# RMS normalization on one core: squares of nine rows at the end of the third slot, gamma in five pieces, and the last tile stored in halves

## Chip, core and metric

The kernel runs on one core of a Trainium2 chip. The metric is the device time of one execution in microseconds (us), the median of several runs. Tile numbers in the code count from 0; and groups are named by the code's pair (tile, first row).

## What is computed

Each row of 512 float32 numbers is divided by the root of its mean square plus 1e-5, and multiplied by gamma.

```python
batch, seq, dim = 16, 1024, 512
x     : float32 [16, 1024, 512]      # 33.55 MB
gamma : float32 [512]

rms = np.sqrt(np.mean(x ** 2, axis=-1, keepdims=True) + 1e-5)
return x / rms * gamma               # 33.55 MB again
```

The 16384 rows are four tiles of 128 partitions x 32 rows x 512 elements, 8.39 MB each. One row on all 128 partitions is 262 KB.

## The kernel before

Three slots of SBUF hold a tile each; the fourth tile goes into the first slot again once the first tile has been stored from there. All transfers are issued by SyncE, in the order in which the code has them.

```python
slots = [const.tile([P, R, D], fp32, name=f"slot{i}") for i in range(3)]
...
pieces = (0, 128, 192, 256, 320, 384, 448, D)

load(0, 0, 0, 8)                       # tile 0, slot 0, rows 0 to 7
for c0, c1 in zip(pieces, pieces[1:]): # seven transfers of gamma
    nc.sync.dma_start(out=gamma_row[:, c0:c1], in_=gamma.unsqueeze(0)[:, c0:c1])
load(0, 0, 8, 16)
load(0, 0, 16, 32)
load(1, 1, 0, 16)
load(1, 1, 16, 32)
```

The work is cut into nine groups: tile, first row, rows, the pieces in which the sums of squares are formed, and the number of rows at the group's end that GpSimd scales.

```python
groups = [
    (0, 0, 7, (7,), 3),
    (0, 7, 9, (4, 5), 5),
    (0, 16, 16, (7, 5, 4), 7),
    (1, 0, 16, (7, 5, 4), 7),
    ...
    (3, 16, 16, (7, 5, 4), 5),
]

def square_sums(ss, t, g, r, m, k):
    # the pieces take turns between a buffer in PSUM (7 rows) and one in SBUF (5 rows)
    home, name, most = ((psum, "sq_psum", 7), (const, "sq_sbuf", 5))[k % 2]
    sq = home.tile([P, most, D], fp32, name=name)
    rows = slots[slot_of[t]][:, g + r : g + r + m, :]
    nc.scalar.activation(out=sq[:, :m], in_=rows, func=AF.Square)
    nc.vector.tensor_reduce(out=ss[:, r : r + m, 0], in_=sq[:, :m], axis=..., op=OP.add)

def inverse_rms(ss, n):                # ScalarE: square root; VectorE: reciprocal
    ...
def scale_by_pool(rstd, t, g, n, share):
    # GpSimd multiplies the group's last rows by 1/rms, then by gamma_b
    ...
def scale(rstd, t, g, r0, r1):         # ScalarE, one row an instruction
    ...
def times_gamma(t, g, r0, r1):         # VectorE multiplies those rows by gamma_psum
    ...
def transfers(t, g):                   # issued when group (t, g) has been recorded
    if (t, g) == (0, 0):
        store(0, 0, 0, 1)
        load(2, 2, 0, 16)
        store(0, 0, 1, 2)
        load(2, 2, 16, 32)
    elif (t, g) == (0, 16):
        store(0, 0, 2, 16)
        store(0, 0, 16, 32)
        load(3, 0, 0, 16)
        load(3, 0, 16, 32)
    elif (t, g) == (1, 16):
        store(1, 1, 0, 32)
    elif (t, g) == (2, 16):
        store(2, 2, 0, 32)
    elif (t, g) == (3, 16):
        store(3, 0, 0, 32)
```

In the loop, the squares of the next group are formed beside the scaling of this one:

```python
for k, group in enumerate(groups):
    ...
    scale_by_pool(rstd, t, g, n, share)
    for piece in todo[:2]:             # of the next group
        square_sums(*piece)
    scale(rstd, t, g, 0, half)
    if not ahead:                      # the last group
        times_gamma(t, g, 0, half)
    for piece in todo[2:]:
        square_sums(*piece)
    scale(rstd, t, g, half, mine)
    times_gamma(t, g, 0 if ahead else half, mine)
    transfers(t, g)
    for nxt in ahead:
        rstd = inverse_rms(ss, nxt[2])
```

In the compiled program each transfer signals one of eight semaphores, which are taken in turn. A transfer's instruction on SyncE waits until the transfer eight places earlier, which has the same semaphore, has landed. SyncE works through its list strictly in order. This is the beginning of the list:

```
load  tile 0 rows 0-7
load  gamma, seven pieces
load  tile 0 rows 8-15      [waits for semaphore 0]
load  tile 0 rows 16-31     [waits for semaphore 1]
load  tile 1 rows 0-15      [waits for semaphore 2]
load  tile 1 rows 16-31     [waits for semaphore 3]
store tile 0 row 0          [waits for semaphore 4, VectorE]
```

Of the kernel before, what the change touches and what calls it, by code (L numbers as in the profile page):

```python
# [9 lines left out]
def kernel(  # L10
# [7 lines left out]
    P = nc.NUM_PARTITIONS  # L18
    eps = 1e-5
    fp32 = mybir.dt.float32  # L20
# [5 lines left out]
    N, D = xf.shape  # L26
# [9 lines left out]
    const = ctx.enter_context(tc.tile_pool(name="const", bufs=1))  # L36
    stats = ctx.enter_context(tc.tile_pool(name="stats", bufs=9))
    psum = ctx.enter_context(tc.tile_pool(name="psum", bufs=1, space=bass.MemoryType.PSUM))

    slots = [const.tile([P, R, D], fp32, name=f"slot{i}") for i in range(3)]  # L40
# [3 lines left out]
    def load(t, slot, r0, r1):  # L44
        dma = nc.sync.dma_start(out=slots[slot][:, r0:r1], in_=xv[t][:, r0:r1])  # L45
        before_scale.append((slot, r0, r1, dma))

    def store(t, slot, r0, r1):
        dma = nc.sync.dma_start(out=ov[t][:, r0:r1], in_=slots[slot][:, r0:r1])  # L49
        before_scale.append((slot, r0, r1, dma))  # L50

    gamma_row = const.tile([1, D], fp32)
    pieces = (0, 128, 192, 256, 320, 384, 448, D)

    load(0, 0, 0, 8)
    for c0, c1 in zip(pieces, pieces[1:]):
# [15 lines left out]
    nc.scalar.activation(out=table, in_=eps_t, func=AF.Sqrt)  # L72


    groups = [
        (0, 0, 7, (7,), 3),
        (0, 7, 9, (4, 5), 5),
        (0, 16, 16, (7, 5, 4), 7),
        (1, 0, 16, (7, 5, 4), 7),
        (1, 16, 16, (7, 5, 4), 7),  # L80
        (2, 0, 16, (7, 5, 4), 7),
        (2, 16, 16, (7, 5, 4), 7),
        (3, 0, 16, (7, 5, 4), 7),
        (3, 16, 16, (7, 5, 4), 5),
    ]
    slot_of = [0, 1, 2, 0]

    def square_sums(ss, t, g, r, m, k):
        home, name, most = ((psum, "sq_psum", 7), (const, "sq_sbuf", 5))[k % 2]
        sq = home.tile([P, most, D], fp32, name=name)  # L90
        rows = slots[slot_of[t]][:, g + r : g + r + m, :]
        nc.scalar.activation(out=sq[:, :m], in_=rows, func=AF.Square)  # L92
        nc.vector.tensor_reduce(  # L93
            out=ss[:, r : r + m, 0], in_=sq[:, :m], axis=mybir.AxisListType.X, op=OP.add
        )

    def inverse_rms(ss, n):
        nc.scalar.activation(out=ss[:, :n, 0], in_=ss[:, :n, 0], func=AF.Sqrt, bias=eps_t, scale=1.0 / D)  # L98
        nc.vector.reciprocal(out=ss[:, :n, 0], in_=ss[:, :n, 0])  # L99
        return ss  # L100

    def scale_by_pool(rstd, t, g, n, share):
        part = slots[slot_of[t]][:, g + n - share : g + n, :]
        by_row = rstd[:, n - share : n].to_broadcast([P, share, D])
        nc.gpsimd.tensor_tensor(out=part, in0=part, in1=by_row, op=OP.mult)  # L105
        last = nc.gpsimd.tensor_tensor(  # L106
            out=part, in0=part, in1=gamma_b.to_broadcast([P, share, D]), op=OP.mult
        )
        before_scale.append((slot_of[t], g + n - share, g + n, last))

    def scale(rstd, t, g, r0, r1):
        x = slots[slot_of[t]]
        for r in range(r0, r1):
            nc.scalar.activation(out=x[:, g + r, :], in_=x[:, g + r, :], func=AF.Copy, scale=rstd[:, r])  # L114

    def times_gamma(t, g, r0, r1):
        part = slots[slot_of[t]][:, g + r0 : g + r1, :]
        scaled = nc.vector.tensor_tensor(  # L118
            out=part, in0=part, in1=gamma_psum.to_broadcast([P, r1 - r0, D]), op=OP.mult
        )  # L120
        for slot, b0, b1, earlier in before_scale:
            if slot == slot_of[t] and b0 < g + r1 and g + r0 < b1:
                tc.declare_no_dep(scaled.ins, earlier.ins, reason="ScalarE waited for it before it scaled these rows")

    def transfers(t, g):
        if (t, g) == (0, 0):
            store(0, 0, 0, 1)
            load(2, 2, 0, 16)
            store(0, 0, 1, 2)
            load(2, 2, 16, 32)  # L130
        elif (t, g) == (0, 16):
            store(0, 0, 2, 16)
            store(0, 0, 16, 32)
            load(3, 0, 0, 16)
            load(3, 0, 16, 32)
        elif (t, g) == (1, 16):
            store(1, 1, 0, 32)
        elif (t, g) == (2, 16):
            store(2, 2, 0, 32)
        elif (t, g) == (3, 16):  # L140
            store(3, 0, 0, 32)

    def pieces_of(group):
        t, g, n, pieces, share = group
        ss = stats.tile([P, 16, 1], fp32, name="ss")
        r = 0
        todo = []
        for k, m in enumerate(pieces):
            todo.append((ss, t, g, r, m, k))
            r += m  # L150
        return ss, todo

    ss, todo = pieces_of(groups[0])
    for piece in todo:
        square_sums(*piece)
    rstd = inverse_rms(ss, groups[0][2])
    nc.scalar.copy(out=gamma_b[:, 0], in_=gamma_psum[:, 0])  # L157
    for k, group in enumerate(groups):
        t, g, n, pieces, share = group
        mine = n - share  # L160
        half = (mine + 1) // 2
        ahead = groups[k + 1 :][:1]
        ss, todo = pieces_of(ahead[0]) if ahead else (None, [])
        scale_by_pool(rstd, t, g, n, share)
        for piece in todo[:2]:
            square_sums(*piece)
        scale(rstd, t, g, 0, half)
        if not ahead:
            times_gamma(t, g, 0, half)
        for piece in todo[2:]:  # L170
            square_sums(*piece)
        scale(rstd, t, g, half, mine)
        times_gamma(t, g, 0 if ahead else half, mine)
        transfers(t, g)
        for nxt in ahead:
            rstd = inverse_rms(ss, nxt[2])
# [30 lines left out]
```

## Time and profile before

| | |
|---|---|
| time, median of 3 runs | 163.77 us (163.73 to 164.01) |
| span of the profiled execution | 162.0 us |
| bytes moved | 67.12 MB, mean 414 GB/s over the span |
| VectorE busy | 111.5 us (69%) |
| ScalarE busy | 107.0 us (66%) |
| GpSimd busy | 110.3 us (68%) |
| TensorE busy | 2.0 us (1%) |

In the profile's lines PE is TensorE, DVE VectorE, ACT ScalarE, POOL GpSimd and SP SyncE; SPq is SyncE's queue of instructions, and L45, L49 and L57 are the lines of the kernel that load, store and fetch gamma. The table of slices cuts the span into 40 equal parts, with the busy share in tenths. In a table of windows, each row is a stretch of time with its length, the busy time of each engine, the granted TensorE clock, the mean busy share of the 16 transfer engines and the GB/s that they moved; a packet is counted where it ends. In a timeline, the first number is the start, the second the time until the last of the merged instructions ended.

### The profile page before, as it was taken

How to read it: one execution, taken by the hardware profiler on the slowest of the kernel's cores; microseconds unless marked ns; L12 is line 12 of the kernel's file. 1: busy time of each engine (PE TensorE's matmuls, PEld its weight loads, DVE VectorE, ACT ScalarE, POOL GpSimd, SP SyncE). 2: the span in 40 equal slices, each digit the busy share in tenths (PEclk: the TensorE clock that was granted, in tenths of full speed). 3: DMA queues.
4: the chain of work that ended last, by engine and by line, in shares of the span. 5: the costliest groups of instructions: out<-in, count | busy, mean ns of one | idle time of the engine just before them, and what ended most of it. 6: DMA issues, size and time to landing. Idle time of an engine off the chain costs nothing.

```text
span 162.0 us, 278 instructions
## 1 busy us (share of the span) xinstructions
PE 2.0 (1%) x2; PEld 0.5 (0%) x2; DVE 111.5 (69%) x43; ACT 107.0 (66%) x109; POOL 110.3 (68%) x24
## 2 busy tenths in 40 slices
PE   0050000000000000000000000000000000000000
PEld 0010000000000000000000000000000000000000
DVE  0027692997989999999999989899998193000000
ACT  3072968878999998999899499999951950000000
POOL 1001947972999599999999999999999994000000
DMA  6789899899899989999999989959959959959974
GB/s 196 324 291 485 388 453 453 388 469 437 316 509 405 453 388 395 446 453 396 510 388 429 477 388 437 599 259 518 518 259 518 518 259 518 518 259 518 518 324 194
DMA packets 2319, 67.12 MB, mean 414 GB/s; under 512 B 269, under 2 KB 270, under 8 KB 526
## 3 DMA queue, kind: packets, MB, share of 16 engines
q1 hardware_dynamic: 2318, 67.11, 97.1%
q14 instruction: 1, 0.01, 0.0%
HBM read 33.56 MB, written 33.55 MB: 414 GB/s over the span
## 4 chain that ended last, share of the span: by engine, by line
DMA 48%; POOL 11%; DVE 10%; ACT 8%; POOLq 4%; issue 2%; SPq 0%; ACTq 0%
DMA slot<-in_x_dram 27%; DMA out_dram<-slot 21%; POOL slot L105 7%; DVE ss L93 5%; POOL slot L106 5%; DVE slot L118 4%; POOLq L202 3%; ACT slot L114 3%; ACT sq_psum L92 3%; ACT sq_sbuf L92 1%; SPq L45 0%; DVE ss L99 0%; SPq L49 0%; POOLq L105 0%; ACTq L92 0%
## 5 line engine op out<-in xcount | busy, mean ns | idle before, releaser
L105 POOL TENSOR_TENSOR slot<-slot,ss 128x3584 f32<-128x3584 f32 (+2 forms) x9 | 48.7, 5407 | 24.0 <-DVE ss L99 24.0
L93 DVE TENSOR_REDUCE ss<-sq_psum 128x7 f32<-128x3584 f32 (+1 forms) x16 | 49.2, 3074 | 18.8 <-ACT sq_psum L92 18.8
L106 POOL TENSOR_TENSOR slot<-slot,gamma_b 128x3584 f32<-128x3584 f32 (+2 forms) x9 | 61.4, 6826 | 0.7
L114 ACT ACTIVATE slot<-slot,ss 128x512 f32<-128x512 f32 x73 | 46.2, 706 | 4.7 <-DVE ss L99 4.7
L92 ACT ACTIVATE sq_psum<-slot 128x3584 f32<-128x3584 f32 (+1 forms) x16 | 40.2, 2512 | 10.6 <-DMA slot<-in_x_dram 9.2
L118 DVE TENSOR_TENSOR slot<-slot,gamma_psum 128x4608 f32<-128x4608 f32 (+3 forms) x10 | 40.3, 4042 | 4.2 <-ACT slot L114 4.2
L93 DVE TENSOR_REDUCE ss<-sq_sbuf 128x5 f32<-128x2560 f32 x8 | 22.5, 2809 | 0.0
L92 ACT ACTIVATE sq_sbuf<-slot 128x2560 f32<-128x2560 f32 x8 | 18.6, 2320 | 0.0
L98 ACT ACTIVATE ss<-ss,eps_t 128x16 f32<-128x16 f32 (+2 forms) x9 | 2.7, 302 | 8.4 <-DVE ss L93 8.4
L99 DVE RECIPROCAL ss<-ss 128x16 f32<-128x16 f32 (+2 forms) x9 | 2.1, 238 | 0.4 <-ACT ss L98 0.4
L66 PE MATMUL gamma_psum<-gamma_row,ones_col 1*128 1x512 f32 x2 | 2.0, 1122 | 9.0 <-DMA gamma_row<-in_gamma_dram 9.0
L72 ACT ACT_TABLE_LOAD x1 | 1.3, 1283 | 1.1 <-PEq L191 1.1
L157 ACT COPY gamma_b<-gamma_psum 128x512 f32<-128x512 f32 x1 | 0.6, 566 | 0.0
L66 PEld LDWEIGHTS gamma_psum<-gamma_row,ones_col 1*128 1x128 f32 x2 | 0.5, 305 | 9.0 <-issue 9.0
L64 POOL MEMSET ones_col<- 1x128 f32 x1 | 0.2, 195 | 0.3 <-POOLq L191 0.3
L191 POOL MEMSET const-float32-0.0<- 128x1 f32 x1 | 0.1, 99 | 0.2 <-issue 0.2
L72 ACT ACTIVATE table<-eps_t 128x1 f32<-128x1 f32 x1 | 0.2, 203 | 0.0
L191 POOL MEMSET const-bfloat16-1.0<- 128x1 bf16 x1 | 0.1, 102 | 0.0
L191 POOL MEMSET const-uint8-127<- 128x1 uint8 x1 | 0.1, 102 | 0.0
L191 POOL MEMSET const-float32-1.0<- 128x1 f32 x1 | 0.1, 99 | 0.0
L70 POOL MEMSET eps_t<- 128x1 f32 x1 | 0.1, 89 | 0.0
## 6 DMA issues: line engine op xcount, KB each, us to landing
slot<-in_x_dram SPq DMA_DIRECT2D x7, 4096.0 KB
slot<-in_x_dram SPq DMA_DIRECT2D x2, 2048.0 KB, 7.3
out_dram<-slot SPq DMA_DIRECT2D x1, 4096.0 KB
out_dram<-slot SPq DMA_DIRECT2D x1, 3584.0 KB, 34.7
out_dram<-slot SPq DMA_DIRECT2D x2, 256.0 KB
gamma_row<-in_gamma_dram SPq DMA_DIRECT2D x6, 0.2 KB
out_dram<-slot SPq DMA_DIRECT2D x3
gamma_row<-in_gamma_dram SPq DMA_DIRECT2D x1, 0.5 KB
```

The lines of the kernel that those rows point to most:

```text
L66: nc.tensor.matmul(gamma_psum[:, 0], ones_col, gamma_row, start=True, stop=True)
L72: nc.scalar.activation(out=table, in_=eps_t, func=AF.Sqrt)
L92: nc.scalar.activation(out=sq[:, :m], in_=rows, func=AF.Square)
L93: nc.vector.tensor_reduce(out=ss[:, r : r + m, 0], in_=sq[:, :m], axis=mybir.AxisListType.X, op=OP.add)
L98: nc.scalar.activation(out=ss[:, :n, 0], in_=ss[:, :n, 0], func=AF.Sqrt, bias=eps_t, scale=1.0 / D)
L99: nc.vector.reciprocal(out=ss[:, :n, 0], in_=ss[:, :n, 0])
L105: nc.gpsimd.tensor_tensor(out=part, in0=part, in1=by_row, op=OP.mult)
L106: last = nc.gpsimd.tensor_tensor(out=part, in0=part, in1=gamma_b.to_broadcast([P, share, D]), op=OP.mult)
L114: nc.scalar.activation(out=x[:, g + r, :], in_=x[:, g + r, :], func=AF.Copy, scale=rstd[:, r])
L118: scaled = nc.vector.tensor_tensor(out=part, in0=part, in1=gamma_psum.to_broadcast([P, r1 - r0, D]), op=OP.mult)
L157: nc.scalar.copy(out=gamma_b[:, 0], in_=gamma_psum[:, 0])
L202: with _tile.TileContext(nc) as tc:
```

## The change

The squares of nine rows at once need 18 KB in each partition, for which there is no buffer. Until the last nine rows of tile 2 are loaded, the end of the third slot is free; the change lets the groups (0,7), (0,16) and (1,0) write squares there, so that each has one piece less, and splits the load of tile 2 so that these rows come after their last use as a buffer. A third row of tile 0 is stored alone ahead of that load. Gamma comes in five pieces. At the end the last tile is stored in two halves, the last group gives GpSimd three rows where it had five, and its multiplication by gamma is one instruction.

```diff
-    pieces = (0, 128, 192, 256, 320, 384, 448, D)
+    pieces = (0, 128, 224, 320, 416, D)
 ...
         (0, 0, 7, (7,), 3),
-        (0, 7, 9, (4, 5), 5),
-        (0, 16, 16, (7, 5, 4), 7),
-        (1, 0, 16, (7, 5, 4), 7),
+        (0, 7, 9, (9,), 5),
+        (0, 16, 16, (7, 9), 7),
+        (1, 0, 16, (7, 9), 7),
 ...
-        (3, 16, 16, (7, 5, 4), 5),
+        (3, 16, 16, (7, 5, 4), 3),
 ...
-        home, name, most = ((psum, "sq_psum", 7), (const, "sq_sbuf", 5))[k % 2]
-        sq = home.tile([P, most, D], fp32, name=name)
+        if m == 9:
+            sq = slots[2][:, 23:32, :]
+        else:
+            home, name, most = ((psum, "sq_psum", 7), (const, "sq_sbuf", 5))[k % 2]
+            sq = home.tile([P, most, D], fp32, name=name)
 ...
             store(0, 0, 0, 1)
             load(2, 2, 0, 16)
             store(0, 0, 1, 2)
-            load(2, 2, 16, 32)
+            load(2, 2, 16, 23)
         elif (t, g) == (0, 16):
-            store(0, 0, 2, 16)
+            store(0, 0, 2, 3)
+            load(2, 2, 23, 32)
+            store(0, 0, 3, 16)
             store(0, 0, 16, 32)
 ...
+        elif (t, g) == (3, 0):
+            store(3, 0, 0, 16)
         elif (t, g) == (3, 16):
-            store(3, 0, 0, 32)
+            store(3, 0, 16, 32)
 ...
         scale(rstd, t, g, 0, half)
-        if not ahead:
-            times_gamma(t, g, 0, half)
         for piece in todo[2:]:
             square_sums(*piece)
         scale(rstd, t, g, half, mine)
-        times_gamma(t, g, 0 if ahead else half, mine)
+        times_gamma(t, g, 0, mine)
```

SyncE's list in the changed program, as compiled (its beginning and its middle):

```
load  tile 0 rows 0-7
load  gamma, five pieces
load  tile 0 rows 8-15
load  tile 0 rows 16-31
load  tile 1 rows 0-15      [waits for semaphore 0]
load  tile 1 rows 16-31     [waits for semaphore 1]
store tile 0 row 0          [waits for semaphore 2, VectorE]
load  tile 2 rows 0-15      [waits for semaphore 3]
store tile 0 row 1          [waits for semaphore 4, ScalarE]
load  tile 2 rows 16-22     [waits for semaphore 5]
store tile 0 row 2          [waits for semaphore 6, ScalarE]
load  tile 2 rows 23-31     [waits for semaphore 7, VectorE]
store tile 0 rows 3-15      [waits for semaphore 0, GpSimd]
store tile 0 rows 16-31     [waits for semaphore 1, VectorE, GpSimd]
```

## The prediction

> **What bounds the kernel now.** I read the page's 40 slices first, then the queues, then the windows of the transfer engines, and the chain of waits last.
>
> The DMA row of the slices and the queue line say what the kernel is made of:
>
> ```profile
> DVE  0027692997989999999999989899998193000000
> ACT  3072968878999998999899499999951950000000
> POOL 1001947972999599999999999999999994000000
> DMA  6789899899899989999999989959959959959974
> ...
> q1 hardware_dynamic: 2318, 67.11, 97.1%
> ```
>
> VectorE, ScalarE and GpSimd each work for about two thirds of the span and have nothing to do in its last 26 us; the transfers go on from the first slice to the last. 67.11 MB is the input and the output once each, so no byte can go. (A dip to 5 followed by 9 is counting: a packet is booked where it ends.) The question is therefore whether the stream has holes. Stretches of the stream (the last two columns are the DMA share and GB/s):
>
> ```profile
> 3.25:7.00 3.75, 0.00 (x0) 0.00 (x0) 0.00 (x0) 0.00 (x0) 0.00 (x0) 1.00 1.01 433
> 7.00:7.25 0.25, 0.00 (x0) 0.00 (x0) 0.00 (x0) 0.00 (x0) 0.00 (x0) 1.00 0.16 66
> 7.25:8.75 1.50, 0.00 (x0) 0.00 (x0) 0.00 (x0) 0.72 (x1) 0.00 (x0) 1.00 0.01 1
> 8.75:9.25 0.50, 0.25 (x1) 0.28 (x2) 0.00 (x0) 0.50 (x1) 0.00 (x0) 1.00 1.91 426
> 9.25:10.25 1.00, 1.00 (x2) 0.21 (x2) 0.00 (x0) 1.00 (x1) 0.00 (x0) 1.00 0.36 115
> ...
> 12.00:40.00 28.00, 0.00 (x0) 0.00 (x0) 21.87 (x11) 20.25 (x18) 16.77 (x5) 1.00 1.02 439
> 40.00:64.00 24.00, 0.00 (x0) 0.00 (x0) 22.87 (x9) 23.07 (x26) 22.12 (x4) 1.00 1.02 427
> 64.00:91.00 27.00, 0.00 (x0) 0.00 (x0) 27.00 (x10) 25.93 (x26) 26.84 (x5) 1.00 0.99 427
> 91.00:121.00 30.00, 0.00 (x0) 0.00 (x0) 28.88 (x12) 26.27 (x27) 29.68 (x5) 1.00 1.01 437
> 121.00:158.50 37.50, 0.00 (x0) 0.00 (x0) 10.13 (x4) 6.85 (x11) 14.49 (x3) 1.00 1.03 447
> ```
>
> From 12 us to 158.5 us the rate never leaves 427 to 447 GB/s: no hole there. There is exactly one hole, between 7 and about 10 us. The order of issues on SyncE explains it:
>
> ```profile
> 0.74 0.38 SPq L45 DMA_DIRECT2D slot<-in_x_dram  x1
> 1.18 2.36 SPq L57 DMA_DIRECT2D gamma_row<-in_gamma_dram  x7
> 8.02 1.86 SPq L45 DMA_DIRECT2D slot<-in_x_dram  x4
> ```
>
> SyncE has nothing to do from 3.54 to 8.02 us, and the second load goes out just as the first has landed (0.74 + 7.26 = 8.00 in the chain of waits). The compiled list of SyncE's instructions says why: transfers use eight semaphores in turn, one load and seven pieces of gamma use up all eight, and the ninth transfer, which is the load of rows 8 to 15, waits for the first transfer's semaphore.
>
> **What the Trainium skill says.** "DMA: Bandwidth & Descriptors", section "Where 436 GB/s comes from", gives 435.2 GB/s as the ceiling of the SBUF ports. The 433 to 439 GB/s above agree; I take it that the stream cannot go faster. The same page's "Anatomy of one DMA — SWDGE (gpsimd) path" says that a wait is made by the issuing sequencer and that the transfer engines merely consume their queues: so what costs time is a queue that runs empty, and a late issue into a full queue costs none. The trace agrees: loads issued at 25 us disturb nothing. Its "Latency and other measured facts" has about 0.6 us to the first byte and a longer receipt after the last. Here the first load's bytes end at about 7.2 us and its semaphore comes at 8.0 (0.8 us), and the first packets after the issue at 8.02 are booked at 8.75 to 9.25 us. Both latencies together make the hole.
>
> **The change, part by part.**
>
> 1. *Gamma in five pieces for seven.* One load and five pieces are six transfers, so the loads of rows 8 to 15 and 16 to 31 are the seventh and eighth; in the new list they wait for nothing. Seven pieces took 2.36 us from 1.18 us, 0.34 each, so the two loads go out at about 2.9 and 3.3 us, long before the queue is empty at 7.1. The first transfer that now waits for the first load is the load of tile 1, at about 8 us, while the 6.29 MB of those two loads are in the queue. The hole is gone. Its size: a straight line through the cumulative bytes from 3.2 to 7.1 us (434 GB/s) reaches zero at 2.24 us. Lines from 12 to 40 us (435 GB/s) and from 122 to 158 us (433 GB/s) reach it at 4.48 and 4.36 us. The stream is shifted by 2.1 to 2.2 us, and the line from the end gives the same as that from just after the hole: nothing else is lost between. **Saving 2.2 us.**
>
> 2. *Nine-row squares in the third slot.* Groups (0,7), (0,16) and (1,0) each lose one ScalarE and one VectorE instruction. From the mean durations of 7, 5 and 4 rows (VectorE 3861, 2809, 2286 ns; ScalarE 3148, 2320, 1875 ns), a row costs about 525 and 420 ns and an instruction about 0.19 and 0.2 us besides. So nine rows take about 4.9 and 4.0 us, and each group saves 0.2 us on each engine. But the overlap gets coarser: in (0,7) the sum of 9 rows starts when all nine are squared, at 19.85 us instead of 17.73, and ends at 24.8 instead of 22.80. Followed through: multiplication by gamma to 27.1, reciprocal to 27.3 (25.12 before); in (0,16) ScalarE squares 25.1 to 28.3 and 28.3 to 32.3, VectorE sums to 37.2, multiplies to 39.5, reciprocal 39.75 (39.40 before); in (1,0) squares to 44.7, sum to 49.7, reciprocal 55.65 (55.16 before). The engines gain nothing early and are 0.5 us late. None of it is on the path: the last store of before is issued at 135.6 us, when the engines are done, and its 8.39 MB begin to move at 158.5 - 8.39/0.435 = 139.2 us, 3.6 us later. A delay of 0.5 us lies within that.
>
> 3. *The load of the last nine rows of the third slot comes after the squares.* It waits for the sum of (1,0), 49.7 us, and everything behind it waits in order. Before it, 25.2 - 2.36 MB of loads and three rows stored (0.79 MB) are issued, 23.6 MB; with 2.1 MB done at 7.1 us, the rest at 435 GB/s lasts until 7.1 + 21.5/0.435 = 56.5 us. The issue has 6.8 us in hand, or about 5.8 after the time to the first byte. Cost: 0.
>
> 4. *One row more stored alone.* 256 KB in 2 KB packets. The two such rows before fell inside a stretch whose line shows no loss; I allow 0.1 us.
>
> 5. *Last tile stored in two halves, GpSimd's share of the last group 3, the last multiplication in one.* ScalarE scales 13 rows, 13 x 0.623 = 8.1 us, then VectorE multiplies 6656 elements, about 7.1 us (2278 ns for 2048, 4949 for 4608). From a reciprocal at about 125.4 us the last store is issued at 140.7 us in place of 135.6. The stream should end 2.1 us earlier than before, at 158.5 - 2.1 = 156.4 us; its last 4.19 MB take 9.6 us, so the queue holds the store of tile 2 until 137.2 and then the first half of tile 3 (ready at about 126) until 146.8 us: 6.1 us in hand. Cost 0; an end with 32 KB packets instead of 64 KB may move it by some tenths.
>
> Sum: 163.77 - 2.2 + 0.1 = 161.7 us, 1.3%. All that the title speaks of is beside the path; the gain comes from the gamma pieces alone.
>
> **The rivals.**
>
> *The stream runs dry where it now waits for VectorE* (parts 3 and 5). Against it: 6.8 and 6.1 us in hand, worked out above. For it: the engines are 0.5 us later, and a first load whose receipt is delayed by the traffic behind it could add 1 us. Each microsecond beyond the margin would be lost one for one; I see 163 us or more only if the nine-row pieces are several microseconds dearer than the fit.
>
> *The hole is worth more, or less.* If engines after the hole lose more than the shift of the lines shows, 2.6 us (161.2); if most of the second start-up (115 GB/s from 9.25 to 10.25 us) belongs to any first packets and appears again when the load of rows 8 to 15 follows, only 1.6 us (162.2).
>
> *The engines bound the time and fewer sums help.* Then 3 x 0.2 us would come off as well, but the last 26 us without any engine at work speak against it: 0.
>
> *Smaller packets and more transfers slow the stream.* 1% of the rate in the affected 20 MB is 0.5 us: 162.2.
>
> **Range and chances.** 161.7 us, 161.0 to 162.6. Faster by over 2% needs 160.5 us, a saving of 3.3 us where the lines show 2.2: 0.06. Slower needs a dry queue of over 5 us: 0.02. Within 2%: 0.92.
>
> **What would show it.** Right: SyncE issues three loads before 4 us; 400 GB/s or more in each stretch from 7 to 12 us; the load of rows 23 to 31 issued near 50 us and the last store near 140 us without a fall in the rate; the stream ends near 156.4 us; the reciprocal of (0,7) comes 2 us later and that of (1,0) 0.5 us. Wrong: a stretch of low rate near 52 to 58 or 138 to 148 us, or a hole at 7 to 9 us that stays.

## The result

The changed kernel takes 161.3 us (161.22 to 161.34) against 163.75 us before: a ratio of 0.985, with a 95% interval of 0.983 to 0.986. That is 2.45 us less, or 1.5%.

The page of the changed kernel first, the rows that answer to those of before: the slices of the three engines and of the transfers, and the transfer queue.

```profile
DVE  0028097998898999999999999999999009700000
ACT  3072957967999998999899899989960990000000
POOL 1000942994999599999999999999999990000000
DMA  5999999999999999999999999996996997999995
...
q1 hardware_dynamic: 2746, 67.11, 98.2%
```

The DMA row has its first 9 in the second slice; before, it took until the fourth. The engines again have nothing to do in the last five slices or more (six before), while the transfers go on. In the windows over the first 12 us (last two columns: DMA share and GB/s) the hole is gone:

```profile
7.00:7.25 0.25, 0.00 (x0) 0.00 (x0) 0.00 (x0) 0.00 (x0) 0.00 (x0) 1.00 0.47 197
7.25:8.75 1.50, 0.06 (x1) 0.10 (x1) 0.00 (x0) 0.87 (x1) 0.00 (x0) 1.00 1.16 493
8.75:9.25 0.50, 0.50 (x1) 0.40 (x2) 0.00 (x0) 0.50 (x1) 0.00 (x0) 1.00 0.84 360
9.25:10.25 1.00, 1.00 (x2) 0.00 (x0) 0.00 (x0) 1.00 (x1) 0.00 (x0) 1.00 0.88 377
10.25:12.00 1.75, 0.48 (x1) 0.00 (x0) 0.93 (x1) 0.79 (x1) 0.00 (x0) 1.00 1.00 431
```

Where 1 GB/s stood from 7.25 to 8.75 us there are 493.

The tables of windows must be read differently from what was said ahead: a packet is counted, with all its bytes and all its time, in the stretch in which it starts, not in that in which it ends. A line of before shows it:

```profile
8.75:9.00 0.25, 0.00 (x0) 0.03 (x1) 0.00 (x0) 0.25 (x1) 0.00 (x0) 1.00 0.59 131
```

131 GB/s in 0.25 us are two packets of 16 KB, and 0.59 of 16 engines for 0.25 us are 1.18 us for each. If they had ended before 9.00 us, they would have begun before 7.82 us, ahead of their issue at 8.02. They start in this stretch. With each packet's bytes spread over its own time in the trace, the changed kernel moves 428 to 432 GB/s in all five stretches above; before moves 50, 54 and 218 GB/s in the second to fourth, and nothing from 7.62 to 8.99 us.

SyncE's timeline has the reason: the second and third load follow gamma at once (two of the four loads in the third line have been issued by 3.74 us).

```profile
0.74 0.38 SPq L45 DMA_DIRECT2D slot<-in_x_dram  x1
1.18 1.68 SPq L57 DMA_DIRECT2D gamma_row<-in_gamma_dram  x5
2.90 5.78 SPq L45 DMA_DIRECT2D slot<-in_x_dram  x4
...
49.40 0.33 SPq L45 DMA_DIRECT2D slot<-in_x_dram  x1
```

The last line is the load that waits for the sum of nine rows. The last store is issued at 138.76 us.

Adding up windows of a quarter of a microsecond gives the moment at which the stream has moved so many bytes. The distance between two kernels is then the time that one has gained by that point:

```
MB moved                         3      11      31      51      63     67.1 (last start)
before, at us                  11.59   29.47   76.84  122.00  150.56   158.48
changed kernel, us earlier      2.47    2.49    2.45    2.58    2.37     1.29
```

All of the gain is there by 3 MB, and it hardly grows or shrinks until 63 MB. The last column, the last start of a packet with data, looked like a puzzle: there the lead is only 1.29 us, though the whole kernel ends 2.4 us earlier (span 159.6 against 162.0). This was the reason for the second theory below. The trace has the answer: the last packets hold 64 KB and take 2.42 us before, and hold 32 KB and take 1.21 us in the changed kernel, so that the data end at 160.76 and 158.37 us, 2.39 us apart. With the bytes spread over each packet's time the lead is 2.41 us at 3 MB and between 2.4 and 2.5 us to the end, but for 2.3 to 2.4 us from 21 to 25 MB.

The page's chain of waits would mislead here:

```profile
DVE 59%; ACT 22%; DMA 4%; ACTq 0%; issue 0%
```

In before it began "DMA 48%". It ends at 138.7 us with VectorE's last multiplication, which released the last store; the 20 us of transfers after it are not in it, and the shares add up to 85%. It names the engine that issued last, not what set the end. SyncE's own waits have the rest, waits at the end for stores to land:

```profile
SPq L208 <- DMA out_dram<-slot: 19.4, 3, 9.6
```

### The profile page after: what moved, and what is told of

The parts are those of the page before. It is cut to its first block, busy times and chain, and to the rows that moved or that the text cites. A ratio compares the mean times of both kernels' runs of the same rounds, so it can differ in the third digit from the quotient of the medians.

```text
span 159.6 us, 275 instructions
## 1 busy us (share of the span) xinstructions
PE 2.0 (1%) x2; PEld 0.5 (0%) x2; DVE 112.0 (70%) x39; ACT 107.8 (68%) x108; POOL 106.4 (67%) x24
## 4 chain that ended last, share of the span: by engine, by line
DVE 59%; ACT 22%; DMA 4%; ACTq 0%; issue 0%
DVE ss L97 36%; DVE slot L122 23%; ACT slot L118 8%; ACT slot L96 7%; ACT sq_psum L96 6%; DMA slot<-in_x_dram 4%; DVE ss L103 1%; ACT ss L102 1%; ACTq L208 0%; ACT gamma_b L165 0%
## 5 line engine op out<-in xcount | busy, mean ns | idle before, releaser
L109 POOL TENSOR_TENSOR slot<-slot,ss 128x3584 f32<-128x3584 f32 (+2 forms) x9 | 46.9, 5214 | 23.7 <-DVE ss L103 23.7
L110 POOL TENSOR_TENSOR slot<-slot,gamma_b 128x3584 f32<-128x3584 f32 (+2 forms) x9 | 59.3, 6585 | 0.7
L97 DVE TENSOR_REDUCE ss<-sq_psum 128x7 f32<-128x3584 f32 (+1 forms) x13 | 42.2, 3246 | 13.2 <-ACT sq_psum L96 13.2
L118 ACT ACTIVATE slot<-slot,ss 128x512 f32<-128x512 f32 x75 | 47.2, 706 | 4.7 <-DVE ss L103 4.7
L122 DVE TENSOR_TENSOR slot<-slot,gamma_psum 128x4608 f32<-128x4608 f32 (+2 forms) x9 | 41.3, 4590 | 8.7 <-ACT slot L118 8.7
L96 ACT ACTIVATE sq_psum<-slot 128x3584 f32<-128x3584 f32 (+1 forms) x13 | 34.6, 2658 | 6.0 <-DMA slot<-in_x_dram 5.2
L97 DVE TENSOR_REDUCE ss<-slot 128x9 f32<-128x4608 f32 x3 | 14.9, 4953 | 4.4 <-ACT slot L96 4.2
L97 DVE TENSOR_REDUCE ss<-sq_sbuf 128x5 f32<-128x2560 f32 x5 | 14.0, 2802 | 0.0
L96 ACT ACTIVATE slot<-slot 128x4608 f32<-128x4608 f32 x3 | 12.1, 4032 | 0.0
L96 ACT ACTIVATE sq_sbuf<-slot 128x2560 f32<-128x2560 f32 x5 | 11.6, 2320 | 0.0
```

The costliest lines, as they stand in the source:

```text
L110: last = nc.gpsimd.tensor_tensor(out=part, in0=part, in1=gamma_b.to_broadcast([P, share, D]), op=OP.mult)
L122: scaled = nc.vector.tensor_tensor(out=part, in0=part, in1=gamma_psum.to_broadcast([P, r1 - r0, D]), op=OP.mult)
```

## The experiments

**Theory A**: only an empty transfer queue costs time; the hole was all there was to gain, and gamma's pieces removed it. **Theory B**: the hole gave 1.4 us, as the last column above was read, and the smaller packets of the last stores gave 1.0. **Theory C**: fewer sums give a part.

These runs were timed in three sets, in which before took 163.92, 164.03 and 164.26 us, so the ratio to before within each set is what counts. The changed kernel's 0.985 would be 161.4 to 161.75 us there. In the expectations, "booked end" is the last start of a packet, and "receipt" the time from there to the signal.

### Gamma in five pieces alone

```diff
-    pieces = (0, 128, 192, 256, 320, 384, 448, D)
+    pieces = (0, 128, 224, 320, 416, D)
```

> Before, with gamma in five pieces and nothing else changed. Theory A (the whole gain is the hole that the eight semaphores make at 7 us): 163.75 - 2.45 = 161.3 us, the time of the changed kernel, and the cumulative stream 2.4 to 2.5 us ahead of before at every byte from 5 MB to the end. Theory B (the hole gives 1.4 us, by which the booked end of the stream moved from 158.5 to 157.1, and the smaller packets of the last stores give the other 1.0, by which the last receipt shortened from 2.0 to 0.9 us): 162.3 us. Theory C (the fewer sums on VectorE and ScalarE give a part): above 161.6 us.

161.55 us, ratio 0.987 (0.985 to 0.989). The stream is 2.41, 2.48, 2.25, 2.39 and 2.26 us ahead of before at 3, 11, 31, 51 and 63 MB, and 2.49 at the last start (64 KB packets in both). One line gives the gain of the whole change within the uncertainty. B's 162.3 us, a ratio of 0.991, lies outside the interval.

### All of the change but the gamma pieces

```diff
-    pieces = (0, 128, 224, 320, 416, D)
+    pieces = (0, 128, 192, 256, 320, 384, 448, D)
```

> The changed kernel with gamma in seven pieces again: all of the change but the gamma pieces. Theory A: 163.7 us, the time of before within 0.3. Theory B: 1.0 us less, 162.7. Theory C: 163 or less.

164.05 us, ratio 1.0005 (0.9995 to 1.0015). The nine-row squares, the split load, the third single row, the halves and GpSimd's smaller share together change the time by no more than 0.15% either way; what each does alone is not shown, save for the halves and the single rows below. C falls, and B's 1.0 us for the halves is not there either. The windows show the hole again:

```profile
7.25:8.75 1.50, 0.00 (x0) 0.00 (x0) 0.00 (x0) 0.87 (x1) 0.00 (x0) 1.00 0.01 1
8.75:9.25 0.50, 0.31 (x1) 0.34 (x2) 0.00 (x0) 0.50 (x1) 0.00 (x0) 1.00 2.25 524
9.25:10.25 1.00, 1.00 (x2) 0.15 (x1) 0.00 (x0) 1.00 (x1) 0.00 (x0) 1.00 0.51 197
```

### The last tile in halves alone

```diff
+        elif (t, g) == (3, 0):
+            store(3, 0, 0, 16)
         elif (t, g) == (3, 16):
-            store(3, 0, 0, 32)
+            store(3, 0, 16, 32)
```

> Before, with the last tile stored in two halves, the first as soon as its group is done. Theory A: the shorter receipt after the last booked packet is only bookkeeping (a packet of 64 KB is booked as ended about 1.2 us further ahead of its write than one of 32 KB): booked end 159.6 us, receipt 0.9 us later, time 163.75 +- 0.2. Theory B: the smaller packets drain sooner, 162.7 us.

163.87 us, ratio 0.9995 (0.9987 to 1.0004): no gain, and B falls. The tail shows again how packets are counted. Before, whose last packets hold 64 KB:

```profile
158.00:158.50 0.50, 0.00 (x0) 0.00 (x0) 0.00 (x0) 0.00 (x0) 0.00 (x0) 1.00 3.32 1442
...
160.00:160.50 0.50, 0.00 (x0) 0.00 (x0) 0.00 (x0) 0.00 (x0) 0.00 (x0) 1.00 0.01 0
160.50:161.00 0.50, 0.00 (x0) 0.00 (x0) 0.00 (x0) 0.00 (x0) 0.00 (x0) 1.00 0.01 0
```

With halves, 32 KB a packet:

```profile
159.50:160.00 0.50, 0.00 (x0) 0.00 (x0) 0.00 (x0) 0.00 (x0) 0.00 (x0) 1.00 2.43 1049
...
160.50:161.00 0.50, 0.00 (x0) 0.00 (x0) 0.00 (x0) 0.00 (x0) 0.00 (x0) 1.00 0.01 0
```

In the first line of before, 1442 GB/s in 0.5 us are eleven packets of 64 KB, and 3.32 of 16 engines are 2.41 us for each. The small share of 0.01 with no bytes is the signal of the landed store. In the trace the 16 last packets of before start from 157.88 to 158.34 us, take 2.42 us each, and their signals come from 160.30 to 160.75 us, each within 0.01 us of a packet's end. With halves the same holds for 1.21 us: the data end, and the signals come, up to 161.16 us. So no delay beside the transfer itself is seen between the last start and the signal, and the last starts of streams with packets of different size can't be compared. Theory A's time was right; its reason, an end booked ahead of the write, was not. (In this run the first load landed later and the second was issued at 8.45 us instead of 8.02, so that its stream lies about 0.4 us behind that of before.)

### The last store in three parts

```diff
-            store(3, 0, 16, 32)
+            store(3, 0, 16, 24)
+            store(3, 0, 24, 28)
+            store(3, 0, 28, 32)
```

> The changed kernel with its last store cut into 8, 4 and 4 rows, so that the last packets are of 8 KB and not of 32 KB. If only the booking of packets changes with their size: 161.3 within 0.2, the booked end of the stream a little later and the receipt after it shorter. If the last packets have to drain: 0.3 to 0.9 us less, 160.4 to 161.0.

161.78 us, ratio 0.985 (0.984 to 0.987), as the changed kernel. The last packet with data starts at 158.34 us (157.16 in the changed kernel) and takes 0.31 us, where one of 32 KB takes 1.21 us: the data end at 158.65 us. Smaller last packets bring nothing.

### Six, eight and one piece of gamma

```diff
-    pieces = (0, 128, 192, 256, 320, 384, 448, D)
+    pieces = (0, 128, 208, 288, 368, 448, D)            # six
+    pieces = (0, 128, 192, 256, 320, 384, 416, 448, D)  # eight
+    pieces = (0, D)                                     # one
```

> Before, with gamma in six pieces. Seven transfers come ahead of the load of rows 8 to 15, so that it takes the eighth semaphore and goes out at once; only the load of rows 16 to 31 waits for the first load, and by then 2.1 MB (4.8 us) are in the queue. Theory A (an empty queue is what costs): the whole gain, the time of five pieces, 161.5 us. If each piece of gamma costs a like amount: half of the gain, 162.7 us.

> Before, with gamma in eight pieces. Theory A: now the eighth piece waits for the first load, and the load of rows 8 to 15 follows one issue later, at 8.4 us in place of 8.02: the hole grows by about 0.4 us, 164.15 us. If instead each piece of gamma costs the stream a like amount (two pieces fewer gave 2.45 us), one more costs 1.2 us: 165.0.

> Before, with gamma in one piece. Theory A: the time of five pieces, 161.5 us within 0.3: there is one hole to remove, and five pieces have removed it. If each piece costs, a further gain of over 1 us.

```
pieces   second load issued at us   ratio to before (95% interval)
1              1.55                 0.986  (0.985 to 0.987)
5              2.92                 0.987  (0.985 to 0.989)
6              3.21                 0.987  (0.985 to 0.989)
7              8.02                 1
8              8.19                 1.0012 (1.0005 to 1.0019)
```

A step, not a slope: the time depends on whether the second load takes one of the first eight semaphores, and not on the number of small transfers. One load of 2.1 MB ahead of the wait is enough. With eight pieces the loss is 0.2 us where 0.4 was expected; the second load was issued only 0.17 us later, since the piece of gamma that now goes first went out at 7.93 us and took 0.22 us to issue:

```profile
7.93 0.22 SPq L57 DMA_DIRECT2D gamma_row<-in_gamma_dram  x1
8.19 0.83 SPq L45 DMA_DIRECT2D slot<-in_x_dram  x2
```

### One group further, the load first or the stores first

Both kernels give group (1,16) the nine-row squares as well, so that VectorE has one instruction fewer and the load of tile 2's last rows waits until about 63.8 us. They differ in one thing: whether the stores of tile 0 stand behind the waiting load or ahead of it.

```diff
-        (1, 16, 16, (7, 5, 4), 7),
+        (1, 16, 16, (7, 9), 7),
 ...
             store(0, 0, 2, 3)
+        elif (t, g) == (1, 0):            # load first
             load(2, 2, 23, 32)
             store(0, 0, 3, 16)
             store(0, 0, 16, 32)
 ...
             store(0, 0, 2, 3)
+            store(0, 0, 3, 16)            # stores first
+            store(0, 0, 16, 32)
+        elif (t, g) == (1, 0):
             load(2, 2, 23, 32)
-            store(0, 0, 3, 16)
-            store(0, 0, 16, 32)
```

> The changed kernel, with the change carried one group further: group (1,16) also writes the squares of nine rows to the end of the third slot, so that the load of tile 2's last nine rows, with the stores of tile 0 behind it, waits for that group's sum. VectorE has one instruction fewer. Sum of nine rows ends at about 63.8 us; the 23.6 MB issued before end at about 57.2 us. Theory A: the queue is empty from 57.2 us, and since the hole of before cost 1.55 us more than the time from its last byte (7.1) to the next issue (8.02), this one costs 63.85 - 57.2 + 1.55 = 8.2 us: 169.5 us. If the margins of the prediction mean nothing and fewer sums help: 161.3 or less.

> The same computation and the same transfers as the run with the load first, but the stores of tile 0's rows 3 to 31 are issued ahead of the waiting load. They are ready at 39 and 55 us, so 7.6 MB lie in the queue while the load waits. Theory A: 161.3 us, as the changed kernel, within 0.3: neither the wait of the load nor one more sum saved is seen. If the later load itself matters: between 162 and 169.

Load first: 170.68 us, ratio 1.041 (1.039 to 1.042). Stores first: 161.8 us, ratio 0.988 (0.985 to 0.990). Same computation, same bytes, 8.9 us apart. The windows with the load first:

```profile
57.25:57.75 0.50, 0.00 (x0) 0.00 (x0) 0.50 (x1) 0.50 (x2) 0.50 (x1) 1.00 0.53 201
57.75:64.25 6.50, 0.00 (x0) 0.00 (x0) 6.50 (x3) 5.44 (x11) 6.42 (x2) 1.00 0.00 0
64.25:65.00 0.75, 0.00 (x0) 0.00 (x0) 0.75 (x1) 0.75 (x1) 0.75 (x1) 1.00 0.81 197
65.00:66.00 1.00, 0.00 (x0) 0.00 (x0) 1.00 (x1) 1.00 (x1) 1.00 (x1) 1.00 0.67 184
66.00:68.00 2.00, 0.00 (x0) 0.00 (x0) 2.00 (x1) 2.00 (x2) 2.00 (x1) 1.00 1.03 424
68.00:72.00 4.00, 0.00 (x0) 0.00 (x0) 4.00 (x3) 4.00 (x6) 4.00 (x2) 1.00 0.99 295
```

and two of the same stretches with the stores first:

```profile
57.75:64.25 6.50, 0.00 (x0) 0.00 (x0) 6.50 (x3) 5.44 (x11) 6.42 (x2) 1.00 0.95 410
...
68.00:72.00 4.00, 0.00 (x0) 0.00 (x0) 4.00 (x3) 4.00 (x6) 4.00 (x2) 1.00 0.99 426
```

All engines work alike in both (the busy columns are equal), and 6.5 us of nothing stand against 410 GB/s. At 25 MB the stream with the load first is 7.99 us behind the changed kernel, where 8.2 were expected; by 27 MB it is 9.20, and then it stays. The further 1.2 us is the stretch from 68 to 72 us: (426 - 295)/426 of 4 us. There the transfer engines count as fully busy at 295 GB/s: the 18 KB packets that start in it took 0.99 us on average, where the fastest took 0.69; why is open. It accounts for the 0.9 us by which the run came out above what was expected of it (a ratio of 1.041 for 1.035).

### Rows stored alone

```diff
-            store(0, 0, 3, 16)            # seven single rows
+            for r in range(3, 7):
+                store(0, 0, r, r + 1)
+            store(0, 0, 7, 16)
 ...
-            store(0, 0, 0, 1)             # no single row
-            store(0, 0, 1, 2)
-            store(0, 0, 2, 3)
             load(2, 2, 23, 32)
-            store(0, 0, 3, 16)
+            store(0, 0, 0, 16)
```

> The changed kernel with four more rows of tile 0 (rows 3 to 6) stored one by one, 256 KB each in 2 KB packets: seven such stores in place of three. The prediction allowed 0.1 us for such a row: 161.7. Theory A with the stream at its ceiling whatever the packets: 161.3 within 0.2. If 2 KB packets run at half the rate: 0.6 us a row, 163.7.

> The changed kernel without any row of tile 0 stored alone: rows 0 to 15 go out in one store after the load of tile 2's last rows. Allowance of the prediction: 161.0. Theory A: 161.3 within 0.2.

Four more single rows: 162.5 us, ratio 0.990 (0.987 to 0.992). None: 162.0 us, ratio 0.987 (0.985 to 0.988). Against the 161.78 us of the changed kernel with its last store cut, which was timed in the same set, the four rows cost 0.7 us or 0.2 each, but taking three away gains nothing. The first misses A's margin, the second misses the gain that an allowance for each row implies. A fixed price for a single row is therefore not shown; the halved rate (0.6 us a row) is excluded. In the trace a 2 KB packet takes 84 ns, which is 390 GB/s over 16 engines, against 432 GB/s for 32 KB packets. From that I estimate 0.07 us more for a row of 256 KB, too little to see.

No kernel tried beats the changed one by more than the uncertainty.

## Why the prediction was right, and where it was off

The prediction was 161.7 us with a range of 161.0 to 162.6; the measurement is 161.3. Its mechanism held: one hole, made by the eight semaphores, and everything else beside the path. Its reading of packets as booked where they end was wrong, and the size of the hole suffered from it. It also says that all the title speaks of is beside the path; the title does name gamma's pieces.

1. *Gamma in five pieces.* Right, and shown by the single edit and by its reverse. The term was mis-sized: 2.2 us predicted, 2.45 measured. The step that failed is the comparison of lines through the stream. Packets are counted where they start; the first load has 16 KB packets of 0.61 us and the later loads 32 KB packets of 1.21 us, so the later line is drawn too early by more than the first. With the bytes spread over the packets' times, the lines of before from 3.2 to 7.1 us and from 12 to 40 us reach zero at 2.53 and 4.96 us, 2.43 apart; in the changed kernel they do so at 2.44 and 2.50. That the line from 122 to 158 us gave the same as the one from 12 to 40 us was luck: spread, it reaches zero at 5.95 us. So something is lost in between (424 GB/s from 40 to 64 us), but the changed kernel loses as much there (425 GB/s).

   The two latencies were misread too. The 0.8 us of receipt were mostly the last packets under way: the last of them ends at 7.62 us, its signal comes at the same moment, and the issue follows 0.40 us later. A separate receipt after the last byte, which the prediction assumed, is not seen. From the issue to the first packet it is 0.97 us (0.61 from the end of the issuing instruction). The rival that the slow second start-up would appear again behind the first load falls: every packet of the second load takes 0.61 us in the changed kernel.

2. *Nine-row squares.* Durations right: VectorE 4953 ns for 4.9 us, ScalarE 4032 ns for 4.0. The reciprocal of (0,7) ends at 27.0 us (27.3 predicted). That of (1,0) ends at 55.05 us (55.65 predicted, 55.16 before), in part because I had let the squares and scalings follow each other by their listed durations, while the timeline has them overlap by 0.06 to 0.10 us each. That the engines' work is off the path is shown by the run without the gamma pieces.

3. *The load that waits for the sum.* Issued at 49.40 us (49.7 predicted), while the queue was still full: its first packet starts at 57.46 us without a gap in the stream, so with the 0.97 us of a start from an empty queue some 7 us were in hand (6.8 or 5.8 predicted). The run with the load first agrees: its wait is 14.5 us longer and costs 8.0 us before the slow stretch, so some 6.5 us were free.

4. *One more row stored alone.* 0.1 us allowed; between nothing and 0.2 us. Too small to tell.

5. *The end.* The last store was issued at 138.76 us (140.7 predicted), since ScalarE no longer waits 1.95 us for tile 3: the transfers run earlier and the reciprocal of the last group starts at 123.23 us, not 125.4. A miss on the safe side, without effect: its first packet starts only at 148.2 us. That 32 KB packets at the end "may move it by some tenths" was unnecessary caution: the halves alone give a ratio of 0.9995.

Of the signs named ahead, three failed as they were worded. The reciprocal of (1,0) came 0.1 us earlier and not 0.5 us later. "400 GB/s or more in each stretch from 7 to 12 us" fails in three of the five as the table counts (197, 360 and 377), though the stream has no hole. And the stream's end "near 156.4 us" was counted at 157.2 us, which would have looked like nearly half of the gain lost. The last two come of the counting alone.

Two points were drawn from the Trainium skill's "DMA: Bandwidth & Descriptors". Its section "Where 436 GB/s comes from" gives a ceiling of 435.2 GB/s, and the traces agree: with the bytes spread, the long stretches of the changed kernel have 425 to 434 GB/s. Its section "Anatomy of one DMA — SWDGE (gpsimd) path" says that the issuing sequencer makes the waits and the transfer engines only consume their queues. That what costs is a queue that runs empty was inferred from it, and the run pair with 8.9 us between them shows that in its plainest form.

## What to carry to other kernels

When transfers set the time, look at the rate over short stretches for holes, and ask of each wait on the issuing queue not how long it is but whether the queue behind it runs empty meanwhile; order the issues so that something ready stands ahead of whatever waits. Count the small transfers ahead of the first large loads, because with eight semaphores taken in turn the ninth waits for the first to land, however small those between are. And try each part of a change by itself: here the squares and the halves did nothing, and one line, gamma in five pieces, did everything.

## What was not expected of the hardware

A store's last signal comes within 0.01 us of the end of its last packet, for packets of 8, 32 and 64 KB alike. The time between the last start and the signal is the packet's own: 0.31, 1.21 and 2.42 us.

An empty queue costs more than the time that it is empty. In the hole of before, between 7 and 12 us, each transfer engine stands idle for 1.77 us on average. Of the second load the first 16 packets of 16 KB then take 1.12 us on average, where 0.61 us is usual; the slow packets cost another 0.59 us, so that 2.36 us are lost in all. With the load first it is 7.49 us of idle engines and again 0.59 us by 67.5 us, before the slow stretch. The first packet starts 0.97 us after the issue in one and 0.96 us in the other. Why the first packets after a pause are slow is not shown.
